# One Trainium2 core, an encoder block: Down's seven-product units spread over two column groups, features loaded in order of use, keys' transpositions kept in place

## The chip, the cores and the metric

The kernel runs on one core of a Trainium2 chip. The core has a matmul engine (PE; its weight loads are listed apart as PEld), a vector engine (DVE), a scalar engine (ACT), a general engine (POOL) and a synchronising engine (SP). SP and POOL issue the DMA transfers here; each has its own queue. Each engine works off its instructions in the order in which they stand in its queue, and semaphores make one engine wait for another.

The metric is the device time of one execution in microseconds (us). One execution was also profiled; the start times below are counted from the start of its span.

## The reference, cut to what matters

One encoder block on 256 positions of width 2048, with a memory of 256 positions. All of it is float32.

```python
mem_n = rms_norm(mem, mem_norm_g)
h = rms_norm(x, norm_g[l, 0])
...
x = x + mix @ w_out[l]
x = x + cross_attention(rms_norm(x, norm_g[l, 1]), mem_n, w_xq[l], w_xkv[l], w_xo[l])
x = x + swiglu(rms_norm(x, norm_g[l, 2]), w_gate_up[l], w_down[l])
return rms_norm(x, final_norm_g)

def swiglu(h, w_gate_up, w_down):
    gate, up = jnp.split(h @ w_gate_up, 2, axis=-1)
    return (jax.nn.silu(gate) * up) @ w_down
```

Two places of it matter below: the keys, `mem_n @ w_xkv[:, :2048]`, and Down, the product `(silu(gate) * up) @ w_down` of 256 x 5632 features with 5632 x 2048 weights. The 5632 features are 44 blocks of 128, called k = 0 to 43.

## The kernel before

**Weights.** All weights lie in device memory as one stream of slabs in the order in which they are used, 128 x 2048 float32 (1 MB) each. SP loads a slab (`raw`, line 128) into one of a few buffers. Every half of it, 128 x 1024, is then split: ACT copies it to a rounded part `wh` (line 148), and DVE subtracts that from the original, which gives the correction `wl` (line 149). A product of features and weights is three matmuls: high by high, high by low, low by high (lines 484, 485 and 486, in `part`). Features and the normed input are split in the same manner.

**Background work.** Work that isn't matmul is written as generators. `Background` (line 236) polls them after the products; a generator's `yield n` asks for n us of pause by a planner's count, and `SOON` is 0.01. So the source decides in which place of the instruction stream a step is written. The instructions of each engine are then ordered by a scheduler that goes by its own estimates; an instruction that was marked with `keep_place` (line 337) stays behind the one that was written before it on its engine. The splits of weights and of plain features in Down are kept in this manner.

**Keys** (lines 654 to 661). The first stage multiplies the normed memory by the key weights in three passes over the columns: the first has columns 0 to 1023 and fills four PSUM banks (`pg`), the second and the third have 512 columns and two banks each. There are four such banks in all. After a pass, `store_turned` (line 509) transposes each bank on DVE (line 513) into a buffer and issues four DMAs on POOL's queue that store it. The next pass takes the bank once its transposition has read it. Beside the passes, a generator computes the scale of the memory's norm: squares on ACT (line 603), their sum on DVE (line 607), and twelve small DVE operations on a 128 x 2 tile (`krc`, in `rstd_cols`, line 369). Background work of other mixers loads tables on SP's queue (lines 1373 to 1379).

**Down** (class at line 1078). The result's columns are four groups of 512. They are worked off in two plans, each for two groups. A plan is a list of slabs, two kinds of them:

- a *plain* slab holds four feature blocks k by one column group: 4 x 2 products (two row halves), 24 matmuls. Plain slabs cover k = 0 to 31, so there are eight for each column group.
- a *unit* holds two blocks k, k + 1 by both column groups, in a form with seven products in place of eight, 21 matmuls. The six units cover k = 32 to 43. A unit needs weights that are sums of blocks (DVE, line 181: one instruction of 1024 columns and two of 512) and a *form* of its two feature blocks (line 1083: four small DVE sums, the splits of both blocks, a split of the 384 summed columns). A unit reads its weights in four pieces, of 512, 1024, 1024 and 1024 columns.

Before, plan one is: the eight plain slabs of group 0, then the first unit, the first plain slab of group 1, the second unit, the second plain slab and so on to the sixth unit, and three plain slabs of group 1. After the last unit, `combine` (line 1137) adds the unit's four own banks into the result on DVE, beside the next plain slab; then `settle` (line 1162) adds the plain banks, beside the rest.

**Features.** Gate-and-up (line 941) stores its transposed output, the features, in device memory in blocks. `fetch` (line 918) brings them back: a DMA on POOL's queue into one of eleven buffers `tmp` (line 926), then a split into a slot (ACT copy at line 319, DVE subtraction at line 311), or for k = 32 and up the form. It keeps some loads ahead of the splits: `ahead` is 3 for the first sixteen features, which are fetched within gate-and-up (line 1022, started with its second group), and 6 for the rest (line 1202). Between two steps it pauses. `ready(k)` (line 1103) runs the fetch forward until `have`, the number of features done, has reached its argument; a plain slab and a unit ask for four features more than the one at hand. The first two slabs of plan one run in `start` (line 1189), while the last background work of gate-and-up ends; the rest in `begin` (line 1198).

Of the kernel before, what the change touches and what calls it, by code (L numbers as in the profile page):

```python
# [22 lines left out]
P = 128  # L23
# [4 lines left out]
FT = DFF // P  # L28
# [26 lines left out]

FORMED = 6

PLAIN = FT - 2 * FORMED


def down_plan():

    units = [("unit", PLAIN + 2 * i) for i in range(FORMED)]
    first, second = ([("plain", c, k) for k in range(0, PLAIN, 4)] for c in range(2))
    mix = lambda a, b: [x for pair in zip(a, b) for x in pair] + a[len(b):]
    one = first + [x for pair in zip(units, second) for x in pair] + second[FORMED:]
    two = first[:1] + mix(first[1:], units) + second
    return one, two

# [1 line left out]
PLANS = down_plan()  # L71

DOWN = GU // 16 + 16 * DFF // 1024

UNITS = {DOWN + i for i, x in enumerate(PLANS[0] + PLANS[1]) if x[0] == "unit"}

# [205 lines left out]
class Block:  # L282
# [223 lines left out]
                    self.bg.poll()  # L506
        return ps

    def store_turned(self, to, u, src):

        nc = self.nc
        self.bg.dve(src.shape[1])
        nc.vector.transpose(u, src)  # L513
        to = to.rearrange("(b f) t -> f b t", f=32)
        for a in range(4):
            nc.gpsimd.dma_start(to[:, :, 32 * a:32 * a + 32],  # L516
                                u[32 * a:32 * a + 32, :].rearrange("f (b t) -> f b t", t=32))
# [48 lines left out]
    def mixers(self):  # L566
# [77 lines left out]
        with tc.tile_pool(name="mid", bufs=1) as mid:  # L644
            self.dgp = mid
            gl = Gla(self, mid)
            with tc.tile_pool(name="hyp", bufs=1) as hyp, tc.tile_pool(name="k2", bufs=8) as k2:
                hy = Hyena(self, hyp, k2)

                mem0 = hy.piece()[:, 0:R + 16]  # L650
                nc.sync.dma_start(mem0, self.t["mem0"])
                self.bg.add(prepare(mid))

                for cols in ([0, 512], [1024], [1536]):
                    first = dict(parts=[[k] for k in range(KT)], before=start_m) if len(cols) > 1 else {}
                    for c, ps in zip(cols, self.gemm_rows("w_xkv", cols, h, **first)):
                        for r in range(2):
                            self.store_turned(self.kd[c:c + 512, r * P:(r + 1) * P], hy.piece(), ps[r][:, :])
                    if first:
                        for k in range(0, KT, 4):  # L660
                            self.load_x(k, 4)
                for hd in range(4):
                    for r, p in enumerate(self.gemm_rows("w_xkv", [D + hd * 512], h, start_x if hd == 3 else rows.append)[0]):
                        for c in range(2):
                            v, o = self.tmp(), (2 * hd + r) * 512 + c * R
                            nc.scalar.activation(v, p[:, c * R:(c + 1) * R], AF.Copy, scale=self.rcm[:, r:r + 1])
                            nc.gpsimd.dma_start(self.vd[:, o:o + R], v)
                self.bg.drain()

                def ev_u(i, p):  # L670
                    hy.feed(i, self.merge(p))
                    if i == 4:
                        self.bg.add(hy.convs())

                self.gemm("w_in", [UH + i * P for i in range(12)], h, ev_u)
                for r, p in enumerate(self.gemm_rows("w_in", [512], h, lambda k: k or low_rank())[0]):
                    nc.scalar.copy(gl.v[r], p)
                self.gemm("w_in", [256, 384, 0, 128], h, lambda i, p: gl.feed(i, self.merge(p)))
                self.gemm("w_in", scols[0:NSC], h, ev_s, narrow=True)
                self.bg.drain()  # L680

            with tc.tile_pool(name="glp", bufs=1) as glp:
                gl.open(glp)
                fn = Fnet(self, glp, act[20:24])
                g_gla = self.bg.add(gl.mix(act[4:8]))
                fn.feed(self.gemm_rows("w_in", [UF], h)[0])
                g_fn = self.bg.add(fn.mix(act[0:4], gl))
                self.gemm("w_in", scols[NSC:], h, lambda i, p: ev_s(i + NSC, p))
                g_sc = self.bg.add(self.group_norm(self.res[1], 2, act[20:24]))

                def ev_gate(i, p):
                    nc.scalar.activation(gl.gate[i], p[:, 0:R], AF.Silu)

                self.gemm("w_in", [1024 + i * P for i in range(4)], h, ev_gate, narrow=True)
                gl.done = True
                self.out_proj(lambda n: [self.bg.drain(g) for g in ((g_gla,), (g_fn, g_sc), ())[n]])
# [218 lines left out]
                    st.places = list(zip(held[0::2], held[1::2]))  # L915
                    d.end()

    def fetch(self, f, k0, k1, ahead, pause, form=None):

        m = {}  # L920
        for k in range(k0, k1 + ahead):
            if k < k1:
                while len(self.stored) <= k // 4:
                    yield
                m[k] = self.tmp()
                self.nc.gpsimd.dma_start(m[k], self.ff[k * P:(k + 1) * P, :])  # L926
            if k >= k0 + ahead:
                i = k - ahead
                if i >= PLAIN:
                    if i % 2:  # L930
                        form(i - 1, m.pop(i - 1), m.pop(i))
                        self.have = i + 1
                        yield pause
                    continue
                mark = self.mark()
                self.split(f[i], m.pop(i))
                self.keep_place(mark)
                self.have = i + 1
                yield pause

    def gate_up(self, sw, gp, f):

        nc, st = self.nc, self.st
        box, self.stored = {}, []
        sums = {}

        def norm():
# [69 lines left out]
        for j in range(DFF // 512):  # L1017
# [1 line left out]
            banks = [self.gbank, self.bank]  # L1019
            cs = [[banks[j % 2]() for _ in cols] for _ in range(2)]  # L1020
            if j == 1:
                early = self.bg.add(self.fetch(f, 0, EARLY, 3, 2.0))
            for i in range(8):
                if j >= NUDGE and i in (2, 4, 7):
                    self.bg.nudge(turned if i == 2 else early)
# [48 lines left out]
class Down:  # L1074
# [27 lines left out]

    def ready(self, k):
        b = self.b
        while b.have < k:
            b.bg.step(next(e for e in b.bg.q if e[0] is self.fetching))

    def part(self, key, *a):
# [5 lines left out]

    def plain(self, c, i, k0):
        for k in range(k0, k0 + 4):
            self.ready(min(len(self.f), k + 4))
            w = self.st.take("w_down", k, (c + i) * 512, 4)
            if c + i == 3 and k >= PLAIN - LATE:
                self.held.append((k, w))  # L1120
                continue
            for r in range(2):
                self.part((i, r), *self.whole(k, r), *w)
# [3 lines left out]

    def unit(self, c, k):

        self.ready(min(FT, k + 4))  # L1130
        formed = lambda n: [self.forms[k][:, a + n * P:a + (n + 1) * P] for a in (0, 384)]
        for (key, a), w in zip((("p1", self.whole(k, 0)), ((1, 0), formed(2)), ((0, 0), self.whole(k + 1, 0)),
                                ("p5", self.whole(k, 1)), ("p7", formed(1)), ("p6", formed(0)), ((0, 1), self.whole(k + 1, 1))),
# [64 lines left out]
    def begin(self, sd):  # L1198

        b = self.b  # L1200
        self.sd = sd
        self.fetching = b.bg.add(b.fetch(self.f, EARLY, FT, 6, SOON, self.form))
        one, two = PLANS
        n, self.rest = (1 + max(i for i, x in enumerate(plan) if x[0] == "unit") for plan in PLANS)
        self.run(0, one[AHEAD:n], b.gbank)
# [643 lines left out]
```

## Time and profile before

| | |
|---|---|
| runs (us) | 1461.06, 1459.96, 1461.03 |
| median (us) | 1461.03 |
| the profiled execution (us) | 1459.79 |
| its span, first to last instruction (us) | 1458.0 |
| mean granted clock of PE | 0.997 |
| weight splits on ACT, line 148 | 589 instructions, 1013 ns mean |
| weight corrections on DVE, line 149 | 589 instructions, 1175 ns mean |
| slab loads on SP | 246 of 1 MB |
| feature loads on POOL, line 926 | 44 of 128 KB |

Rows of a timeline read: start in us, duration in us, engine, line, operation, output<-input, shape; "x3" at the end joins three instructions in a row; a bracket gives the idle time of the engine before it and what ended it. Rows of windows read: window, its length, then busy us (and instructions) of PE, PEld, DVE, ACT and POOL, the granted clock of PE (1.00 is full), the busy share of the DMA engines, and GB/s. In the rows of DMA issues the last number is the median time from issue to landing. PE's neighbouring matmuls overlap in these records, and their ends are modelled.

### The profile page before, as it was taken

To read this page: it belongs to the slowest core of one execution; us is meant where nothing else is said; L and a number is where in the kernel's file an instruction comes from. 1 tells how busy PE (TensorE), PEld (TensorE's weight loads), DVE (VectorE), ACT (ScalarE), POOL (GpSimd) and SP (SyncE) were. 2 spreads that over 40 slices of the span, in tenths; PEclk is the share of its full clock that TensorE was granted. 3 is DMA by queue.
4 is the path that set the end of the run, shared out by engine and by line. 5 is a ranking of instruction groups with operands and counts; after the bars stand their busy time and mean duration, and the time that the engine had idled before them with its cause. 6 is when DMAs were issued, how large, how long until landed. Compare 5 with 4: busy or idle time off the path is not lost.

```text
span 1458.0 us, 19733 instructions
## 1 busy us (share of the span) xinstructions
PE 1441.3 (99%) x7219; PEld 1218.0 (84%) x7219; DVE 1191.4 (82%) x1748; ACT 843.7 (58%) x1252; POOL 172.3 (12%) x294
## 2 busy tenths in 40 slices
PE   9999999999999999999999999999999999899997
PEld 7878888898899888888888888888888888688886
DVE  6587768778868767877778999999999996898875
ACT  6555755466656646765565555555555564555554
POOL 0220100000000001100003344112201113100000
PEclk9999999999999999999999999999999999999999
DMA  9975654454535656545556767666666656465554
GB/s 349 346 263 196 220 210 154 165 180 161 191 130 206 214 178 224 173 171 191 183 203 202 279 240 246 207 219 221 243 218 243 238 204 223 155 229 179 226 203 144
DMA packets 57393, 307.16 MB, mean 211 GB/s; under 512 B 9773, under 2 KB 11470, under 8 KB 25680
## 3 DMA queue, kind: packets, MB, share of 16 engines
q1 hardware_dynamic: 45920, 281.11, 54.3%
q0 software_dynamic: 10944, 24.14, 5.4%
q8 instruction: 56, 0.92, 0.3%
q10 hardware_dynamic: 432, 0.66, 0.1%
q14 instruction: 41, 0.34, 0.1%
HBM read 291.71 MB, written 14.16 MB: 210 GB/s over the span
## 4 chain that ended last, share of the span: by engine, by line
PE 94%; issue 2%; DVE 1%; DMA 1%; POOL 1%; ACT 1%; SPq 0%; DVEq 0%; POOLq 0%; ACTq 0%
PE pg L433 18%; PE pg L485 13%; PE pg L486 13%; PE pg L484 13%; PE pg L434 10%; PE pm L485 6%; PE pm L484 6%; PE pm L486 6%; PE pm L1350 1%; DMA tmp<-hidden 1%; DVE wl L149 1%; PE pg L430 1%; PE pg L431 1%; PE pm L881 1%; PE pm L854 1%
## 5 line engine op out<-in xcount | busy, mean ns | idle before, releaser
L148 ACT CAST wh<-raw 128x1024 fp32r<-128x1024 f32 (+1 forms) x589 | 589.3, 1013 | 475.8 <-PE pg L486 147.8
L149 DVE TENSOR_TENSOR wl<-raw,wh 128x1024 fp32r<-128x1024 f32 (+1 forms) x589 | 681.4, 1175 | 179.4 <-ACT wh L148 173.7
L433 PE MATMUL pg<-act,wh 128*128 128x512 f32 x1104 | 387.6, 393 | 0.0
L434 PE MATMUL pg<-act,wl 128*128 128x256 f32 x1216 | 340.7, 280 | 0.0
L485 PE MATMUL pg<-wl,act 128*128 128x512 f32 (+1 forms) x689 | 268.3, 389 | 3.0 <-DVE wl L149 3.0
L484 PE MATMUL pg<-wh,act 128*128 128x512 f32 (+1 forms) x689 | 268.8, 391 | 0.5 <-ACT wh L148 0.5
L486 PE MATMUL pg<-wh,act 128*128 128x512 f32 (+1 forms) x689 | 268.2, 389 | 0.0
L433 PEld LDWEIGHTS pg<-act,wh 128*128 128x128 f32 x1104 | 207.4, 188 | 44.9
L434 PEld LDWEIGHTS pg<-act,wl 128*128 128x128 f32 x1216 | 228.6, 188 | 0.8 <-DVE wl L149 0.5
L485 PEld LDWEIGHTS pg<-wl,act 128*128 128x128 f32 x689 | 129.5, 188 | 31.3 <-DVE wl L149 4.8
L484 PEld LDWEIGHTS pg<-wh,act 128*128 128x128 f32 x689 | 129.5, 188 | 28.2 <-issue 0.8
L486 PEld LDWEIGHTS pg<-wh,act 128*128 128x128 f32 x689 | 129.4, 188 | 27.3 <-issue 0.4
L484 PE MATMUL pm<-wh,act 128*128 128x512 f32 x318 | 124.5, 391 | 1.2 <-ACT act L319 1.2
L486 PE MATMUL pm<-wh,act 128*128 128x512 f32 x318 | 124.4, 391 | 0.6 <-DVE act L311 0.6
L485 PE MATMUL pm<-wl,act 128*128 128x512 f32 x318 | 124.5, 391 | 0.0
L181 DVE TENSOR_TENSOR raw<-raw 128x1024 f32<-128x1024 f32 x129 | 111.6, 865 | 2.9
L516 POOL DMA_DIRECT2D hidden<-u x88 | 56.8, 653 | 152.5 <-DVE u L513 130.4
L484 PEld LDWEIGHTS pm<-wh,act 128*128 128x128 f32 x318 | 60.1, 189 | 14.2 <-ACT act L319 1.6
L486 PEld LDWEIGHTS pm<-wh,act 128*128 128x128 f32 x318 | 60.1, 189 | 13.5 <-DVE act L311 1.0
L485 PEld LDWEIGHTS pm<-wl,act 128*128 128x128 f32 x318 | 60.0, 189 | 12.5
L1062 POOL DMA_DIRECT2D xrows<-tmp x64 | 37.0, 585 | 184.2 <-DVE rc L315 126.6
L926 POOL DMA_DIRECT2D tmp<-hidden x44 | 24.5, 561 | 151.4 <-DVE f L311 87.4
(353 smaller groups left out, 1773.0 us busy)
## 6 DMA issues: line engine op xcount, KB each, us to landing
raw<-in_W SPq DMA_DIRECT2D x246, 1024.0 KB, 5.0
raw<-in_W SPq DMA_DIRECT2D x11, 512.0 KB, 7.2
hidden<-u POOLq DMA_DIRECT2D x88, 64.0 KB, 4.6
tmp<-hidden POOLq DMA_DIRECT2D x44, 128.0 KB, 4.7
res<-in_xT SPq DMA_DIRECT2D x8, 512.0 KB, 8.3
k<-in_mem SPq DMA_DIRECT2D x8, 256.0 KB, 6.6
k<-in_x SPq DMA_DIRECT2D x8, 256.0 KB, 8.9
keys<-k POOLq DMA_DIRECT2D x32, 64.0 KB, 5.7
```

Of the source, the lines that this page charges most:

```text
L148: nc.scalar.copy(wh[:, a:b], r[:, a:b])
L149: nc.vector.tensor_tensor(out=wl[:, a:b], in0=r[:, a:b], in1=wh[:, a:b].bitcast(F32), op=ALU.subtract)
L181: op = lambda out, a, b, what=ALU.subtract: nc.vector.tensor_tensor(out=out, in0=a, in1=b, op=what)
L430: self.nc.tensor.matmul(p[:, 0:R], wh, slot[:, 0:R], start=start, stop=False)
L433: self.nc.tensor.matmul(p[:, :], wh, slot[:, :], start=start, stop=False)
L434: self.nc.tensor.matmul(p[:, 0:R], wl, slot[:, 0:R], start=False, stop=stop)
L484: self.nc.tensor.matmul(p, hi, wh, start=start, stop=False)
L485: self.nc.tensor.matmul(p, hi, wl, start=False, stop=False)
L486: self.nc.tensor.matmul(p, lo, wh, start=False, stop=stop)
L516: nc.gpsimd.dma_start(to[:, :, 32 * a:32 * a + 32], u[32 * a:32 * a + 32, :].rearrange("f (b t) -> f b t", t=32))
L926: self.nc.gpsimd.dma_start(m[k], self.ff[k * P:(k + 1) * P, :])
L1062: nc.gpsimd.dma_start(to[:, :, c:c + 32], u[32 * a:32 * a + 32, :].rearrange("t (b f) -> t b f", f=32))
```

## The change

Three things change.

1. Plan one's order. Group 0's eight plain slabs and group 1's eight stand in a row, and the units are put in after the fifth, seventh, ninth, eleventh, thirteenth and fourteenth of them (`AFTER`, counted from 0). Plan two, the number of slabs and their contents stay; so does the layout of each slab, while the stream's order follows the plan.
2. `INNER` lists the features in the order in which plan one first uses them: 0 to 19, 32, 33, 20 to 27, 34, 35, 28 to 31, 36 and so on. `fetch` goes by such a list, keeps eight loads ahead instead of six, pauses 0.8 instead of 0.01 after a plain feature and 3.0 after a form; `have` counts features in that order, and `ready(k)` runs the fetch until four more than k's place are done. The sixteen features fetched early are the same. Since the last unit now stands before two plain slabs only, `combine` runs beside the first and `settle` beside the second.
3. The transpositions of the keys are kept at their written place on DVE. In the built program, DVE's queue at the end of the first pass then reads: a weight correction, the sum of line 607, the twelve operations on `krc`, a weight correction, the four transpositions, a weight correction. Before, the first transposition stood after the second of the twelve operations, the other three after the third, and both weight corrections and the other nine operations behind them. At the end of the second pass two weight corrections stood behind the two transpositions; now they stand ahead of them.

```diff
@@ -55,6 +55,8 @@
 
 FORMED = 6
 
+AFTER = (4, 6, 8, 10, 12, 13)
+
 PLAIN = FT - 2 * FORMED
 
 
@@ -63,7 +65,9 @@
     units = [("unit", PLAIN + 2 * i) for i in range(FORMED)]
     first, second = ([("plain", c, k) for k in range(0, PLAIN, 4)] for c in range(2))
     mix = lambda a, b: [x for pair in zip(a, b) for x in pair] + a[len(b):]
-    one = first + [x for pair in zip(units, second) for x in pair] + second[FORMED:]
+    one = []
+    for n, x in enumerate(first + second):
+        one += [x] + [units[i] for i, a in enumerate(AFTER) if a == n]
     two = first[:1] + mix(first[1:], units) + second
     return one, two
 
@@ -71,6 +75,8 @@
 PLANS = down_plan()
 
 DOWN = GU // 16 + 16 * DFF // 1024
+
+INNER = list(dict.fromkeys(k for x in PLANS[0] for k in (range(x[2], x[2] + 4) if x[0] == "plain" else range(x[1], x[1] + 2))))
 
 UNITS = {DOWN + i for i, x in enumerate(PLANS[0] + PLANS[1]) if x[0] == "unit"}
 
@@ -506,11 +512,14 @@
                     self.bg.poll()
         return ps
 
-    def store_turned(self, to, u, src):
+    def store_turned(self, to, u, src, keep=False):
 
         nc = self.nc
         self.bg.dve(src.shape[1])
+        mark = self.mark()
         nc.vector.transpose(u, src)
+        if keep:
+            self.keep_place(mark)
         to = to.rearrange("(b f) t -> f b t", f=32)
         for a in range(4):
             nc.gpsimd.dma_start(to[:, :, 32 * a:32 * a + 32],
@@ -655,7 +664,7 @@
                     first = dict(parts=[[k] for k in range(KT)], before=start_m) if len(cols) > 1 else {}
                     for c, ps in zip(cols, self.gemm_rows("w_xkv", cols, h, **first)):
                         for r in range(2):
-                            self.store_turned(self.kd[c:c + 512, r * P:(r + 1) * P], hy.piece(), ps[r][:, :])
+                            self.store_turned(self.kd[c:c + 512, r * P:(r + 1) * P], hy.piece(), ps[r][:, :], True)
                     if first:
                         for k in range(0, KT, 4):
                             self.load_x(k, 4)
@@ -915,33 +924,34 @@
                     st.places = list(zip(held[0::2], held[1::2]))
                     d.end()
 
-    def fetch(self, f, k0, k1, ahead, pause, form=None):
+    def fetch(self, f, ks, ahead, pause, form=None):
 
         m = {}
-        for k in range(k0, k1 + ahead):
-            if k < k1:
+        for n in range(len(ks) + ahead):
+            if n < len(ks):
+                k = ks[n]
                 while len(self.stored) <= k // 4:
                     yield
                 m[k] = self.tmp()
                 self.nc.gpsimd.dma_start(m[k], self.ff[k * P:(k + 1) * P, :])
-            if k >= k0 + ahead:
-                i = k - ahead
+            if n >= ahead:
+                i = ks[n - ahead]
                 if i >= PLAIN:
                     if i % 2:
                         form(i - 1, m.pop(i - 1), m.pop(i))
-                        self.have = i + 1
-                        yield pause
+                        self.have += 2
+                        yield 3.0
                     continue
                 mark = self.mark()
                 self.split(f[i], m.pop(i))
                 self.keep_place(mark)
-                self.have = i + 1
+                self.have += 1
                 yield pause
 
     def gate_up(self, sw, gp, f):
 
         nc, st = self.nc, self.st
-        box, self.stored = {}, []
+        box, self.stored, self.have = {}, [], 0
         sums = {}
 
         def norm():
@@ -1019,7 +1029,7 @@
             banks = [self.gbank, self.bank]
             cs = [[banks[j % 2]() for _ in cols] for _ in range(2)]
             if j == 1:
-                early = self.bg.add(self.fetch(f, 0, EARLY, 3, 2.0))
+                early = self.bg.add(self.fetch(f, INNER[:EARLY], 3, 2.0))
             for i in range(8):
                 if j >= NUDGE and i in (2, 4, 7):
                     self.bg.nudge(turned if i == 2 else early)
@@ -1102,7 +1112,7 @@
 
     def ready(self, k):
         b = self.b
-        while b.have < k:
+        while b.have < min(INNER.index(k) + 5, len(INNER)):
             b.bg.step(next(e for e in b.bg.q if e[0] is self.fetching))
 
     def part(self, key, *a):
@@ -1114,7 +1124,7 @@
 
     def plain(self, c, i, k0):
         for k in range(k0, k0 + 4):
-            self.ready(min(len(self.f), k + 4))
+            self.ready(k)
             w = self.st.take("w_down", k, (c + i) * 512, 4)
             if c + i == 3 and k >= PLAIN - LATE:
                 self.held.append((k, w))
@@ -1127,7 +1137,7 @@
 
     def unit(self, c, k):
 
-        self.ready(min(FT, k + 4))
+        self.ready(k + 1)
         formed = lambda n: [self.forms[k][:, a + n * P:a + (n + 1) * P] for a in (0, 384)]
         for (key, a), w in zip((("p1", self.whole(k, 0)), ((1, 0), formed(2)), ((0, 0), self.whole(k + 1, 0)),
                                 ("p5", self.whole(k, 1)), ("p7", formed(1)), ("p6", formed(0)), ((0, 1), self.whole(k + 1, 1))),
@@ -1199,7 +1209,7 @@
 
         b = self.b
         self.sd = sd
-        self.fetching = b.bg.add(b.fetch(self.f, EARLY, FT, 6, SOON, self.form))
+        self.fetching = b.bg.add(b.fetch(self.f, INNER[EARLY:], 8, 0.8, self.form))
         one, two = PLANS
         n, self.rest = (1 + max(i for i, x in enumerate(plan) if x[0] == "unit") for plan in PLANS)
         self.run(0, one[AHEAD:n], b.gbank)
```

## The prediction

> **What bounds the kernel now.** I read the page first, then the span cut into windows, then the stretches in which PE is not full.
>
> ```profile
> span 1458.0 us, 19733 instructions
> PE 1441.3 (99%) x7219; PEld 1218.0 (84%) x7219; DVE 1191.4 (82%) x1748; ACT 843.7 (58%) x1252; POOL 172.3 (12%) x294
> PE 94%; issue 2%; DVE 1%; DMA 1%; POOL 1%; ACT 1%; SPq 0%; DVEq 0%; POOLq 0%; ACTq 0%
> ...
> 1250.00:1300.00 50.00, 47.27 (x196) 37.34 (x197) 47.54 (x75) 29.80 (x43) 1.63 (x3) 0.97 0.50 181
> 1300.00:1350.00 50.00, 50.00 (x223) 41.40 (x222) 43.34 (x52) 28.40 (x36) 0.00 (x0) 1.00 0.55 200
> ```
>
> PE is busy for 1441.3 of 1458.0 us and is 94% of the chain that ended last. So the kernel is bound by matmuls, and no edit that keeps them can win more than PE's gaps. The windows (columns: length, busy time and instructions of PE, PEld, DVE, ACT and POOL, granted clock, DMA share, GB/s) place a gap at 1250 to 1300, where Down's seven-product units start; at 1300 to 1350, still in Down, PE is full. The other place is the keys, at 73 to 76 us.
>
> **Down: what the old order loses.** These are PE's matmuls around the switch from group 0's plain slabs to the units, three ACT copies, and windows.
>
> ```profile
> 1210.09 0.39 PE L484 MATMUL pm<-wh,act 128*128 128x512 f32 x1
> 1226.41 0.39 PE L484 MATMUL pm<-wh,f 128*128 128x512 f32 x1
> ...
> 1248.22 0.39 PE L486 MATMUL pm<-wh,f 128*128 128x512 f32 x1
> 1249.83 0.50 PE L484 MATMUL pm<-wh,act 128*128 128x512 f32 x1 [1.22 <-ACT act L319]
> 1251.12 0.51 PE L486 MATMUL pm<-wh,act 128*128 128x512 f32 x1 [0.56 <-DVE act L311]
> 1261.84 0.50 PE L485 MATMUL pg<-wl,act 128*128 128x512 f32 x1 [1.35 <-DVE wl L149]
> 1264.32 0.49 PE L485 MATMUL pg<-wl,s 128*128 128x512 f32 x1 [0.82 <-DVE wl L149]
> 1264.88 0.40 PE L484 MATMUL pm<-wh,act 128*128 128x512 f32 x1
> ...
> 1248.12 0.41 ACT L319 CAST act<-tmp 128x256 fp32r<-128x256 f32 x1 [3.05 <-DMA tmp<-hidden]
> 1256.16 0.41 ACT L319 CAST act<-tmp 128x256 fp32r<-128x256 f32 x1 [3.81 <-DMA tmp<-hidden]
> ...
> 1248.45:1264.89 16.44, 12.49 (x44) 8.82 (x44) 12.92 (x26) 10.94 (x22) 1.63 (x3) 0.90 0.30 105
> 1248.17:1251.58 3.41, 1.63 (x6) 0.72 (x6) 2.07 (x5) 3.36 (x8) 0.22 (x1) 1.00 0.32 103
> 1251.58:1254.99 3.41, 3.41 (x10) 2.63 (x9) 3.41 (x9) 0.71 (x2) 1.34 (x3) 0.50 0.90 322
> 1258.41:1261.82 3.41, 2.08 (x9) 1.11 (x7) 3.41 (x7) 1.84 (x4) 0.00 (x0) 1.00 0.00 0
> ```
>
> 1210.09 and 1226.41 begin the first and the fourth slab, so a plain slab of 24 matmuls takes 16.32 / 3 = 5.44 us, 0.2267 us each. From 1248.22 to 1264.88 there are 44 matmuls (the window's x44 counts both ends), 43 steps: 43 x 0.2267 = 9.75 us of the 16.66 us that pass. So 6.9 us are lost. The four bracketed waits are 3.95 of it; the clock at 0.50 for 3.41 us, after a window in which PE was busy for 1.63 us, costs half of that, 1.7; restarts and small gaps are the rest. Some 0.3 us on either side of the stretch makes **7.5 us** in all. Cause: ACT stands still for 3.05 and 3.81 us behind features that have not landed, since forms and plain features are fetched in numerical order, and the copies and sums of the first units queue behind them. I find no gap of PE from 1264.88 to 1300.
>
> **Down: what the new order costs.** The matmuls are the same in number and kind, only in other places, so PE's work costs nothing more. The same holds for DVE's and ACT's. What moves is when the forms and weight sums fall due. These rows price them.
>
> ```profile
> 1241.28 0.29 DVE L311 TENSOR_TENSOR e<-tmp 128x128 f32<-128x128 f32 x1 [3.54 <-DMA tmp<-hidden]
> 1236.99 0.76 DVE L311 TENSOR_TENSOR f<-tmp,f 128x256 fp32r<-128x256 f32 x2
> 1270.14 0.68 DVE L181 TENSOR_TENSOR raw<-raw 128x512 f32<-128x512 f32 x1
> 1270.74 0.28 DVE L315 SCALAR_TENSOR_TENSOR e<-tmp 128x128 f32<-128x128 f32 x1
> 1232.26 1.08 POOL L926 DMA_DIRECT2D tmp<-hidden  x2 [1.64 <-DVE f L311]
> ...
> tmp<-hidden POOLq DMA_DIRECT2D x2, 128.0 KB, 2.9
> ...
> raw<-in_W SPq DMA_DIRECT2D x246, 1024.0 KB, 5.0
> tmp<-hidden POOLq DMA_DIRECT2D x44, 128.0 KB, 4.7
> ...
> 1235.52 5.74 DMA tmp<-hidden
> ```
>
> One instruction of DVE starts some 0.08 us before the last one ends (1270.14 + 0.68 against 1270.74), so in a row of them a 512 sum counts 0.6, a small sum 0.2, a split of 256 columns 0.34. The row with 2.9 us is the median landing of the loads issued between 1232 and 1233.5; the last row is the longest one in the chain of waits.
>
> Unit 0 now stands after five plain slabs: 1210.09 + 5 x 5.44 = 1237.29. Its 21 matmuls read four pieces of weights; the correction of the fourth piece is first read by the 17th matmul, at 1237.29 + 16 x 0.2267 = 1240.92. On DVE's new queue the first sum of forms 34/35 stands ahead of that piece and waits for a load. From it on DVE needs 2 x 0.2 (that sum and another), 2 x 0.6 (two 512 sums of weights), 4 x 0.34 (splits of plain features) and 2 x 1.16 (corrections of the third and fourth pieces; 2.32 for two in a row of the keys below) = 5.3 us. The load now issues at about 1232.4. Landing in 2.9 us as then and there (1235.3), DVE is held by its own queue till about 1235.8 and the piece is 0.1 late; landing in the usual 4.7 (1237.1) it is 1.5 late. I take 0.2, since the 2.9 row is from the same time and queue.
>
> Unit 1 follows two plain slabs later, at about 1253. Its slab's load is issued once DVE has left unit 0's fourth piece, about 1241.1, and lands at 1246.1 by the 5.0 row. The load of feature 37, issued about 1244.8 and behind it, lands about 1249.5, and its ACT copy stands ahead of unit 1's second piece. From there: that copy 0.4, the weight copy 1.0 (2.00 for two, in the keys' rows), its correction 1.16, two sums 1.2, the form of 36/37 some 2 (four sums, two splits, one split of 384 columns at perhaps 0.5), third and fourth pieces 2.3 = 8.1, so 1257.6 where 1253 + 3.63 = 1256.6 is wanted: 1.0 late. Unit 2 I put at 0.6, an estimate: it comes after as many slabs, and unit 1's wait has given its loads a microsecond. The sum is 1.8, with 0.2 for each of three restarts **2.4 us**. Ends: 1.0 (unit 0 and unit 1 on time but for half a microsecond each) and 5.5 (each load 1 us later). Then Down gains 7.5 - 2.4 = 5.1; I take 4.7, because the slabs loaded after the units come in the same window as the features. Ends: 6.5 and 2. Nothing in the new tail loses PE time: combining group 0 now runs beside one plain slab and settling beside another, the cover that the row 1300 to 1350 shows full with 43 of 50 us on DVE; without it, two 512 adds at 0.7 would be bare. A copy of feature 33 now waits in gate_up for PE, ahead of a weight copy that is held by DVE anyway; nothing.
>
> **Keys.** Here the change takes a wait away and makes another.
>
> ```profile
> 48.89 0.17 DVE L378 TENSOR_SCALAR krc<-krc 128x2 uint32<-128x2 uint32 x1
> 48.97 0.71 DVE L513 STREAM_TRANSPOSE k<-pg 128x512 f32<-128x512 f32 x1
> 49.64 2.08 DVE L513 STREAM_TRANSPOSE k<-pg 128x512 f32<-128x512 f32 x3
> 50.80 0.39 PE L484 MATMUL pg<-wh,act 128*128 128x512 f32 x1
> 51.64 2.32 DVE L149 TENSOR_TENSOR wl<-raw,wh 128x1024 fp32r<-128x1024 f32 x2
> 53.88 0.15 DVE L315 SCALAR_TENSOR_TENSOR krc<-krc 128x2 f32<-128x2 f32 x1
> 55.44 0.16 DVE L315 SCALAR_TENSOR_TENSOR krc<-krc 128x2 f32<-128x2 f32 x1
> ...
> 61.23 3.37 SPq L128 DMA_DIRECT2D raw<-in_W  x3
> 68.94 2.00 ACT L148 CAST wh<-raw 128x1024 fp32r<-128x1024 f32 x2 [1.03 <-DMA raw<-in_W]
> 73.19 1.40 DVE L513 STREAM_TRANSPOSE k<-pg 128x512 f32<-128x512 f32 x2 [2.02 <-PE pg L486]
> 75.75 0.50 PE L485 MATMUL pg<-wl,act 128*128 128x512 f32 x1 [1.47 <-DVE wl L149]
> ```
>
> Before, the first transposition ran at 48.97, in the middle of the small krc operations, and its PSUM bank was free before pass 2's first matmul at 50.80. Kept at its written place, it stands behind all of krc and one weight correction: 48.89 + 0.2 to the next, 0.2 more, then the nine operations that took 53.88 to 55.60, 1.72: 51.0; + 1.16 = 52.15; + 0.71 = 52.85. Pass 2 starts at about 52.95: 2.15 us of idle PE, 2.26 with the restart. The other three transpositions, 0.69 apart, keep pace with a bank per three matmuls (0.68).
>
> At the end of pass 2 the order turns in favour: two corrections now stand ahead of the transpositions which waited 2.02 us for PE. The 1.47 of idle PE at 75.75 goes, 1.7 with its restart. But ACT's chain is 2.2 us later, and behind one of its squares SP's queue holds a table, and then pass 3's first slab: issued at about 66.9, not 61.23. With the old 7.6 us to landing it is there at 74.5, + 1.0 + 1.16 = 76.7 against about 76 wanted (74.1, where the old stall began, and the shift): 0.7 late; with the 5.0 row it is in time. I take 0.35. Keys: 2.26 - 1.73 + 0.35 = **+0.9**, ends +0.5 and +1.3, if the clock stays at 1.00.
>
> The clock may not: a window with 1.63 us of PE went to half speed, one with 2.08 did not (rows above). A stall of 2.15 leaves 1.26 busy in a window of 3.41 us that holds it whole, 1.3 to 2.3 in one that cuts it. The Trainium skill, "TensorE: Matmul & The Clock Gate", section "🔬 Part 1: The HAM clock gate (the "warmup" mystery)", gives the cold state "after ≥1 idle window (~3.4µs)"; by that no stall of 2 us would cost a clock, and the sum would stand. The trace disagrees: 0.50 followed a window with 1.63 us of busy PE.
>
> **Sum.** Against the profiled execution, 1459.79 us (span 1458.0 and 1.8 around it): -4.7 + 0.9 = -3.8, so 1456.0. The median of the runs, 1461.03, lies 1.24 above that execution; 1457.2.
>
> **Rivals.**
> (a) Pass 2's stall drops the clock: 3.41 us at half speed, +1.7: 1458.9. For it the 1.63 row, against it the 2.08 row.
> (b) Slower: the form loads come late. From 5.7 us between issue and landing (the 5.74 row) on, DVE's queue stands behind the load at unit 0: 1232.4 + 5.74 + 5.3 = 1243.4 against 1240.92, 2.5 late. Unit 1, waited for by ACT behind slab and load each about a microsecond later, is 2.4 late, unit 2 about 2. With restarts 0.7 and a half-speed window 1.7 that is 9.3 against the 7.5 lost before; with keys +0.9 and their own half-speed window +1.7 it is 4.4 more: 1465.4. For it: the loads are issued closer together now, eight ahead; against: 2.9 and 4.7.
> (c) The stalls of units 0 to 2 hide entirely: -7.5 + 0.9: 1454.4. Against it: DVE's 5.3 us queue.
> (d) Spreading only moves the gap: the first units stall as before, keys +0.9: 1461.9. For it: the first unit still comes with fetches not done.
>
> **How the numbers follow.** Forecast 0.45, (a) 0.2, (b) 0.15, (c) 0.1, (d) 0.1. A measurement here tells about 0.2% or 2.9 us: faster is below 1458.1, slower above 1464.0. Two thirds of the forecast with (c) and a third of (a) are faster: about 0.52; (b) with a little of (d) 0.17 is slower; the rest 0.31. The range, 1454.6 to 1462.2, reaches from (c) past (d) and leaves (b) out.
>
> **What would show it.** Right: PE idle about 2.1 us at 51 to 53 with DVE's transposition as its releaser, no wait at the end of keys' pass 2 or one under a microsecond, Down's 1237 to 1275 with waits summing to 1 to 3 us and the clock at 1.00. Wrong: waits of ACT or DVE for loaded features over 3 us there, a clock of 0.50 after 53, or a gap at the end of group 1, where combining meets one slab alone.

## The result and the profile after

| | before | after |
|---|---|---|
| median of nine runs each (us) | 1460.0 | 1456.9 |
| lowest and highest | 1459.38 to 1461.09 | 1455.38 to 1460.82 |
| the profiled execution | 1459.79 | 1457.18 |
| its span | 1458.0 | 1455.3 |

The ratio of after to before is 0.9979, 95% interval 0.9969 to 0.9989. That is 3.1 us faster. The median of before had stood at 1461.03 with the three runs that were known first; with six more it is 1460.0.

The page of after, its span, busy times and the shares of the chain that ended last:

```profile
span 1455.3 us, 19732 instructions
PE 1440.2 (99%) x7219; PEld 1217.8 (84%) x7219; DVE 1192.2 (82%) x1748; ACT 844.1 (58%) x1252; POOL 172.2 (12%) x294
...
PE 96%; DVE 2%; ACT 1%; issue 0%; DMA 0%; SPq 0%; ACTq 0%; DVEq 0%
```

The work of each engine is what it was (DVE 1192.2 against 1191.4). What changed is who PE waits for: DMA and "issue", 3% of the chain before, have left it. Line numbers have moved: the weight splits are now lines 154 and 155, the product 490 to 492, the transposition 520, the copy and split of features 325 and 317.

PE's waits in the timeline of after, at the keys and in Down:

```profile
52.78 0.54 PE L490 MATMUL pg<-wh,act 128*128 128x512 f32 x1 [1.99 <-DVE k L520]
53.11 0.63 PE L491 MATMUL pg<-wl,act 128*128 128x512 f32 x1
...
1258.40 0.50 PE L491 MATMUL pg<-wl,act 128*128 128x512 f32 x1 [0.87 <-DVE wl L155]
1260.57 0.50 PE L491 MATMUL pg<-wl,s 128*128 128x512 f32 x1 [0.51 <-DVE wl L155]
...
1275.79 0.50 PE L490 MATMUL pg<-wh,s 128*128 128x512 f32 x1 [0.38 <-ACT wh L154]
```

Before had one wait at the keys (75.75) and four in Down from 1249 to 1265, 3.95 us. Now there are one at the keys, elsewhere, and three in Down, 1.76 us. The one at 52.78 is new, and the matmul behind it takes 0.63 us instead of 0.39: the clock fell. Windows of after:

```profile
49.62:53.04 3.42, 1.43 (x7) 0.92 (x6) 3.21 (x10) 1.64 (x3) 0.10 (x1) 1.00 0.96 348
53.04:56.45 3.41, 3.41 (x9) 2.64 (x9) 3.02 (x6) 0.00 (x0) 3.41 (x6) 0.50 0.94 276
1200.00:1250.00 50.00, 49.96 (x221) 41.05 (x220) 40.90 (x62) 27.13 (x41) 13.91 (x24) 1.00 0.67 229
1250.00:1300.00 50.00, 48.24 (x211) 38.92 (x210) 45.30 (x71) 29.58 (x42) 2.17 (x4) 1.00 0.59 221
```

PE was busy for 1.43 of the 3.42 us up to 53.04, and the next 3.41 us ran at a granted clock of 0.50. In Down the clock stayed at 1.00 and the number of matmuls from 1250 to 1300 rose from 196 to 211.

To see where the difference arises, I matched the starts of the matmuls in the two traces by their number and subtracted. The lag of after is -0.18 us at the 200th matmul (46 us), +1.89 at the 400th, +1.85 at the 6200th (1212 us) and -2.65 at the 6600th; it stays there to the end. So the keys cost **2.07 us**, Down's first plan gained **4.50**, and the rest of the span did nothing. The same two differences (200th to 400th, "keys"; 6200th to 6800th, "Down") are given for each experiment below. The first 24 us vary by up to 1.8 us between these traces, so they are left out of both.

### The profile page after: what moved, and what is told of

It reads as the page before. It is cut to its first block, busy times and chain, and to the rows that moved or that the text cites. A ratio compares the mean times of both kernels' runs of the same rounds, so it can differ in the third digit from the quotient of the medians.

```text
span 1455.3 us, 19732 instructions
## 1 busy us (share of the span) xinstructions
PE 1440.2 (99%) x7219; PEld 1217.8 (84%) x7219; DVE 1192.2 (82%) x1748; ACT 844.1 (58%) x1252; POOL 172.2 (12%) x294
## 4 chain that ended last, share of the span: by engine, by line
PE 96%; DVE 2%; ACT 1%; issue 0%; DMA 0%; SPq 0%; ACTq 0%; DVEq 0%
PE pg L439 19%; PE pg L490 13%; PE pg L491 13%; PE pg L492 13%; PE pg L440 10%; PE pm L490 7%; PE pm L492 7%; PE pm L491 7%; PE pm L1360 1%; DVE wl L155 1%; PE pg L436 1%; PE pg L437 1%; PE pm L890 1%; PE pm L863 1%; ACT wh L154 0%
```

## Experiments

Times are medians; each ratio is to runs of the kernel before on the same chip (median 1460.37 for the first four, 1459.65 and 1459.66 for the others). "Under before" and "over before" are meant against these. Behind the last two columns stands one trace of each kernel. Seven kernels, the change and six of the runs below, have the same plan and the same order of features; their Down still differs by up to 1.6 us, for a reason worked out further below (when one load landed), so smaller differences in that column are not taken for effects.

| run | median (us) | ratio, 95% interval | keys | Down |
|---|---|---|---|---|
| Down alone | 1455.97 | 0.9970, 0.9958 to 0.9981 | -0.03 | -5.15 |
| keys alone | 1461.51 | 1.0008, 0.9999 to 1.0017 | +2.03 | +0.45 |
| first pass free, later passes kept | 1453.84 | 0.9958, 0.9945 to 0.9970 | -1.80 | -4.23 |
| features in numerical order | 1464.26 | 1.0024, 1.0014 to 1.0034 | -0.03 | +3.84 |
| six ahead, no pauses | 1455.03 | 0.9968, 0.9955 to 0.9980 | -0.01 | -5.06 |
| old plan, new fetch | 1458.31 | 0.9989, 0.9980 to 0.9998 | -0.03 | -1.75 |
| second to fourth unit one slab later | 1455.30 | 0.9969, 0.9957 to 0.9980 | -1.81 | -1.27 |
| eight ahead, short pauses | 1454.43 | 0.9960, 0.9947 to 0.9974 | -1.81 | -3.56 |
| later passes kept, six ahead, no pauses | 1453.85 | 0.9961, 0.9948 to 0.9973 | -1.80 | -4.80 |
| first four units one slab later | 1457.97 | 0.9990, 0.9981 to 0.9999 | -1.81 | -1.20 |
| three ahead | 1456.12 | 0.9976, 0.9967 to 0.9984 | -0.03 | -4.38 |

### Down alone and keys alone

Down alone takes the flag away that keeps the keys' transpositions:

```diff
-self.store_turned(self.kd[c:c + 512, r * P:(r + 1) * P], hy.piece(), ps[r][:, :], True)
+self.store_turned(self.kd[c:c + 512, r * P:(r + 1) * P], hy.piece(), ps[r][:, :])
```

> The change to Down and its features alone; the keys' transpositions are free again. By the working of the prediction Down is worth about 4.5 us (the lag of PE's matmuls against before went from +1.85 to -2.65 across Down's first plan), so 4.5 under the kernel before, and all runs close together since no stall at pass 2 is left to touch the clock. Rival: the keys' edit carries part of the gain, then this is less than 3.1 under, the gain of the whole change.

4.4 us under before. The keys' stage is before's again, to 0.03 us. The gain is Down's, and by the traces the whole change gains less than this part of it; the intervals of the two ratios overlap. My second half held less well: the runs spread over 3.3 us, from 1454.14 to 1457.41, all with a recorded mean clock of 0.998 or 0.999, so the touched clock is not the only thing that spreads them.

Keys alone is the kernel before with `store_turned`'s new argument and nothing else:

```diff
+        mark = self.mark()
         nc.vector.transpose(u, src)
+        if keep:
+            self.keep_place(mark)
```

> The keys' edit alone on the kernel before. Theory: a stall of 2.27 us at pass 2's start, minus 1.7 at pass 3's, so 0.4 to 0.6 us over before where the clock stays, and 1.4 more, about 2.1 over, in the runs where the stall drops it; runs spread over some 2 us. Rival: the edit gains, as the wait of 1.47 us at 75.75 goes: 1.5 under.

1.1 us over before by the medians, between the two cases of the theory; the interval touches no change. In its trace the keys cost 2.03 us. PE in the timeline of keys alone:

```profile
53.60 0.48 PE L484 MATMUL pg<-wh,act 128*128 128x512 f32 x1 [1.98 <-DVE k L514]
53.91 0.60 PE L485 MATMUL pg<-wl,act 128*128 128x512 f32 x1
54.30 0.63 PE L486 MATMUL pg<-wh,act 128*128 128x512 f32 x1
```

The same stall and the same half clock behind it as in the kernel with the whole change: two profiled executions of two kernels with this stall, and in both the clock dropped. The rival, that this edit gains, falls.

### Only the later passes kept

```diff
-..., hy.piece(), ps[r][:, :], True)
+..., hy.piece(), ps[r][:, :], not first)
```

> The whole change, but the transpositions of the first pass are free, those of the second and third are kept. Theory: no stall at 52, and no wait of 1.47 us at the end of pass 2: 1.7 under Down alone, so 6.2 under the kernel before. Rival: without the two microseconds of shift the second pass's end meets a slab that has not landed, and the wait stays in another form: the same as Down alone.

6.5 us under before, 2.1 under Down alone (the two intervals overlap, but the traces separate the stages), and the keys' part is -1.80. DVE in its timeline, and the window over the keys:

```profile
48.29 0.17 DVE L384 TENSOR_SCALAR krc<-krc 128x2 uint32<-128x2 uint32 x1
48.37 0.71 DVE L520 STREAM_TRANSPOSE k<-pg 128x512 f32<-128x512 f32 x1
49.01 0.12 DVE L385 TENSOR_SCALAR krc<-krc 128x2 int32<-128x2 int32 x1
49.05 2.08 DVE L520 STREAM_TRANSPOSE k<-pg 128x512 f32<-128x512 f32 x3
...
50.00:100.00 50.00, 50.00 (x220) 40.28 (x219) 35.60 (x72) 27.60 (x43) 17.74 (x29) 1.00 0.84 290
```

The transpositions of the first pass again run ahead of the small operations, and PE is full from 50 to 100 us, where before had 48.53 of 50. So the keys' edit is two edits: at the later passes it takes a stall away, worth 1.8, and at the first it makes one.

### What in Down carries the gain

Numerical order, with the new plan and free keys:

```diff
-INNER = list(dict.fromkeys(k for x in PLANS[0] for k in ...))
+INNER = list(range(FT))
```

> Down's new plan with the features fetched in numerical order (keys free). Theory: the order of use is what makes the early units possible; unit 0 at 1237 then stands behind twelve more plain features and their loads, a stall of 4 to 8 us that takes the 4.5 away: 0 to 4 over before. Rival: spreading the units is what gains, the order of the loads is not: 3 to 4.5 under before.

Slower than before by 3.9 us; Down costs 3.84 in the trace. PE in its timeline:

```profile
1240.77 0.50 PE L490 MATMUL pm<-wh,act 128*128 128x512 f32 x1 [2.29 <-ACT act L325]
1242.25 0.80 PE L492 MATMUL pm<-wh,act 128*128 128x512 f32 x1 [0.57 <-DVE act L317]
1251.25 0.68 PE L490 MATMUL pg<-wh,s 128*128 128x512 f32 x1 [2.98 <-ACT wh L154]
```

Unit 0 now stands where its features are not ready: its first matmul waits for the ACT copy of feature 32. An early unit without early features loses 9 us against one that has them (3.84 against -5.15). Part of it may be the clock: it was at 0.50 from 1241.17 to 1247.99 and from 1251.41 to 1254.82, each time after a wait of PE; how much these 10.2 us cost beside the waits is not shown.

The old plan with the new depth and pauses:

```diff
-for n, x in enumerate(first + second):
-    one += [x] + [units[i] for i, a in enumerate(AFTER) if a == n]
+one = first + [x for pair in zip(units, second) for x in pair] + second[FORMED:]
```

> The old plan (group 0's slabs, then units and slabs in turn) with the new fetch: eight ahead, pauses 0.8 and 3.0, keys free; the order of use is then the numerical one. Theory: the old loss at the switch, 7 us, comes from units that start one slab apart with their forms all at once; two loads more ahead shorten the wait for the first form by some 2 us: 0 to 2.5 under before. Rival: depth and pauses are the cure, not the plan: 4 or more under before.

1.3 us under before, Down -1.75. Depth and pauses alone are not the cure. The old place of the waits remains: they sum to 3.95 us as before, with 1.35 us for the split of a feature at 1253.77 the longest of them. The clock stayed at 1.00.

The new plan with the old depth and pauses:

```diff
-b.fetch(self.f, INNER[EARLY:], 8, 0.8, self.form)
+b.fetch(self.f, INNER[EARLY:], 6, SOON, self.form)
...
-yield 3.0
+yield pause
```

> Down alone (keys free), features in order of use, but fetched as before: six loads ahead, pauses of 0.01. Theory: the order carries the gain, depth and pauses only place the copies and forms between the weights; within 1.5 us of Down alone, so 3 to 5.5 under before. Rival: eight ahead and the pauses are needed, since the early forms' loads come too late with six (the wait for loaded features, 3.9 us in all in the changed kernel, grows): less than 2 under before.

Down is -5.06 against -5.15 of Down alone: once order and plan are there, this depth and these pauses do nothing that can be told. Fewer loads ahead still:

```diff
-b.fetch(self.f, INNER[EARLY:], 8, 0.8, self.form)
+b.fetch(self.f, INNER[EARLY:], 3, 0.8, self.form)
```

> Down alone (keys free) with three feature loads ahead instead of eight, pauses as changed: the loads of the forms come late, the prediction's slower rival made on purpose. If loads that are late by 1 us or more stall units 0 to 2 as I worked out, each unit pays 1.5 to 2.5 us and the clock may drop: 0 to 4 over before, 5 to 8 over Down alone. Rival: forms have slack of a few us, and it costs under 2 against Down alone.

The rival expectation held: Down -4.38, 0.8 less than with eight ahead. ACT's waits for loaded features from 1190 to 1320, in the list of waits of this kernel and of Down alone:

```profile
ACT act L325 <- DMA tmp<-hidden: 4.6, 2, 3.2
```

```profile
ACT act L325 <- DMA tmp<-hidden: 3.8, 2, 2.5
```

The longest wait grew by only 0.7 us, and that is not the setting's doing: the edit did not make the loads late. Less each trace's own lag, the loads of features 20 to 39 go out at the same times with three, six and eight ahead, with and without pauses, to 0.03 us in all seven kernels of this plan and order. POOL's queue waits there for DVE's splits, which free the buffers (the row at 1246.94 further below). So no setting of depth or pauses that was tried moved these loads, and the price of loads late by a whole microsecond at each unit was not measured.

### Attempts at the waits that are left

All four keep the later passes only. Units after the 5th, 8th, 10th, 12th, 13th and 14th slab:

```diff
-AFTER = (4, 6, 8, 10, 12, 13)
+AFTER = (4, 7, 9, 11, 12, 13)
```

> As with the late passes kept and the first free, with units after the 5th, 8th, 10th, 12th, 13th and 14th slab: all plain features come before the second unit. Theory: the waits at units 1 and 2 (1.7 and 0.5 us lost in the changed kernel) come from features that the plain slab between needs as well; with three slabs between units 0 and 1 they shrink below 0.7 in all, 1 to 2 under the same kernel with the change's places. Rival: the last three units one slab apart bring DVE's queue to its limit, as the old plan did, and the loss moves there: 0 or worse.

4.4 us under before where the change's places had 6.5, with overlapping intervals; Down falls to -1.27, outside the 1.6 us of the seven kernels. Not the last units pay, as the rival had it, but unit 1. ACT and PE in its timeline:

```profile
1258.77 0.51 ACT L333 CAST s<-e 128x384 fp32r<-128x384 f32 x1 [1.20 <-DVE e L317]
1259.19 1.04 ACT L154 CAST wh<-raw 128x1024 fp32r<-128x1024 f32 x1
...
1260.28 0.56 PE L490 MATMUL pg<-wh,act 128*128 128x512 f32 x1 [1.88 <-ACT wh L154]
1261.67 0.80 PE L491 MATMUL pg<-wl,act 128*128 128x512 f32 x1 [0.82 <-DVE wl L155]
```

No plain feature is left to fetch between these units, so the forms of the next ones move up, and ACT's copy of one stands ahead of unit 1's weights and waits for DVE. The clock was at 0.50 for 6.83 us from 1260.57 on as well, so part of what is lost there may be its own. The first four units one slab later:

```diff
-AFTER = (4, 6, 8, 10, 12, 13)
+AFTER = (5, 7, 9, 11, 12, 13)
```

> Units after the 6th, 8th, 10th, 12th, 13th and 14th slab (later passes kept, first free, eight ahead). Theory: loads of 36 and 37 are then due one slab later as well, but so are they issued, since DVE's splits free their buffers; the wait at unit 1 stays at 1 to 2 us, within 1 of the run with the change's places. Rival: a slab more before the first unit is 5.4 us of cover, and the waits go: 1.5 to 2.5 under it.

Worse than both expectations: 1.7 us under before, Down -1.20, with waits at units 0 and 1, 4.5 us in all. DVE at its unit 0:

```profile
1239.88 0.29 DVE L317 TENSOR_TENSOR e<-tmp 128x128 f32<-128x128 f32 x1 [3.25 <-DMA tmp<-hidden]
```

DVE's queue stands for 3.25 us behind a form's feature, as it did for 3.54 in the kernel before. Later units do not make earlier features: here the load of feature 34 went out 2.5 us later than in the seven kernels (less the lag), and took 5.93 us to land instead of 2.4 to 2.7. Short pauses with eight ahead:

```diff
-b.fetch(self.f, INNER[EARLY:], 8, 0.8, self.form)
+b.fetch(self.f, INNER[EARLY:], 8, SOON, self.form)
```

> As with the late passes kept and the first free, pauses for plain features 0.01 instead of 0.8, eight ahead. Theory: the load of the second unit's features, issued 3.6 us later than I had estimated, moves forward with the copies; the 1.7 us at unit 1 shrinks: 0.5 to 1.5 under the same kernel with pauses. Rival: copies and splits crowd the weights of gate-and-up's end and unit 0: 0 to 2 over it.

5.2 us under before where the run with pauses had 6.5, with overlapping intervals; Down -3.56 in the trace. The theory's gain is not there, and its premise was wrong: the load issued 3.6 us later than I had estimated (1248.41 against 1244.8) is that of feature 38. The one I had estimated, of feature 37, had gone out at 1246.94, and shorter pauses did not move it. Last, the two best parts together (first pass free, six ahead, no pauses):

> The parts that did best together: first pass's transpositions free, later ones kept, new plan, order of use, six loads ahead without pauses. Theory: the keys' 1.7 us and Down's 4.6 us are in different stages and add up: 6.3 or more under before, equal to or up to 0.5 under the run with eight loads and pauses. Rival: the depth matters only in the noise: the two within 0.3.

5.8 us under before: the stages add up (-1.80 and -4.80), but this is not told apart from the kernel with eight ahead, 1453.84. Both lie below the change itself (ratios 0.9958 and 0.9961 against 0.9979), with intervals that just meet its own, 0.9969 to 0.9989.

## Why the prediction was right, and where not

**What bounds.** PE's gaps were the whole prize. The keys and Down's first plan hold all of the difference; 1000 us of matmuls between them moved by 0.04.

**Down's gain.** Predicted 4.7, measured 4.50 (5.15 in Down alone, 3.56 to 5.06 in the five other kernels with this plan and order). Of the waits worked out in advance:

- Unit 0, predicted 0.2 late with DVE held by its own queue: DVE reached form 34's first sum at 1237.61 without waiting for a load, where I had 1235.8 and the lag of 1.85 comes on top. The unit's 17th matmul started 0.42 us after the one before instead of 0.23, and with the slower next one the unit lost 0.33 (lag 1.85 at the 6330th matmul, 2.18 at the 6340th).

```profile
1237.61 0.28 DVE L317 TENSOR_TENSOR e<-tmp 128x128 f32<-128x128 f32 x1
...
1240.68 1.09 DVE L317 TENSOR_TENSOR f<-tmp,f 128x256 fp32r<-128x256 f32 x3
```

- Unit 1, predicted 1.0 and 0.2 for the restart. Measured: 0.87 + 0.51 of waits, 1.9 by the distances between the matmuls' starts (1.25 and 0.34, 0.90 and 0.34 instead of 0.23). This is the mis-sized term of Down's sum. The path is the one named: ACT's copy of feature 37 stands ahead of the second piece and starts as its load lands.

```profile
1246.94 0.55 POOL L936 DMA_DIRECT2D tmp<-hidden  x1 [3.93 <-DVE f L317]
1248.41 1.08 POOL L936 DMA_DIRECT2D tmp<-hidden  x2 [0.93 <-DVE f L317]
...
1252.24 0.41 ACT L325 CAST act<-tmp 128x256 fp32r<-128x256 f32 x1 [2.85 <-DMA tmp<-hidden]
```

  Counted in the order of use, the load of feature 37 is the one at 1246.94. Less the lag of 1.85 that is 1245.1, where I had about 1244.8; it landed 5.28 us later, where I had 4.7. So ACT's copy comes 0.9 later than worked out, and the unit loses 0.7 more. The working behind it holds: 8.1 us after the copy's start is 1260.3, and the unit's 17th matmul starts at 1260.57.
- Unit 2, put at 0.6 and a restart by an estimate: the wait at 1275.79, 0.64 by the distances.
- The tail, costed at nothing: the lag is -2.65 at the 6600th matmul and at the 7200th. Combining beside one slab costs PE nothing.

The three units lose 2.9 us where 2.4 were put down, out of 7.5 in before; 4.6 is left, and the lag says 4.50. That 4.7 comes so near is partly luck: it holds 0.4 taken off for the slabs loaded after the units, and no loss shows there (the lag is -2.64 at the 6478th matmul and -2.65 at the 6600th), while unit 1 cost 0.7 more than worked out.

The landing of that one load sets what Down gains. In the seven kernels it goes out at the same place, to 0.01 us, units 0 and 2 lose the same to 0.1 us, and unit 1 follows the landing (its loss is taken from the starts of the matmuls 6389 to 6412):

| kernel | load of feature 37, issue to landing (us) | lost at unit 1 (us) | Down |
|---|---|---|---|
| six ahead, no pauses | 4.45 | 1.4 | -5.06 |
| Down alone | 4.49 | 1.3 | -5.15 |
| later passes kept, six ahead, no pauses | 4.84 | 1.7 | -4.80 |
| three ahead | 5.09 | 2.1 | -4.38 |
| the change | 5.28 | 2.0 | -4.50 |
| first pass free, later passes kept | 5.59 | 2.2 | -4.23 |
| eight ahead, short pauses | 6.21 | 2.9 | -3.56 |

Why it lands sooner or later, these runs do not show.

The 7.5 us that before loses are not a sum of waits and a separate price of the clock, as the prediction's first working has it. In keys alone, whose Down is before's, the clock stayed at 1.00 there; PE's waits were 5.01 us instead of 3.95, and Down lost no less, 0.45 us more:

```profile
1250.00:1270.00 20.00, 15.09 (x59) 10.26 (x59) 15.10 (x29) 12.68 (x23) 2.51 (x5) 1.00 0.39 133
```

**Keys.** The stall at pass 2 was worked out as 2.15 us with a first matmul at 52.95; it came at 52.78, and the lag jumped by 2.15 in that step (-0.18 at the last matmul of pass 1, 1.97 at the next). DVE's queue reads as described, with the correction and then all four transpositions behind the small operations:

```profile
50.70 0.16 DVE L321 SCALAR_TENSOR_TENSOR krc<-krc 128x2 f32<-128x2 f32 x1
50.78 1.23 DVE L155 TENSOR_TENSOR wl<-raw,wh 128x1024 fp32r<-128x1024 f32 x1
51.92 2.50 DVE L520 STREAM_TRANSPOSE k<-pg 128x512 f32<-128x512 f32 x4
```

The end of pass 2 gave 1.77 back (3.70 to 1.93) where I had 1.73. Pass 3's first slab was to be 0.35 late: 0. SP's queue behaved as described: the slab's load went out at 68.35, 1.45 after the 66.9 that I had. PE was 1.4 us later by then than my stall alone made it (lag 3.70 against 2.26), by the half clock; that this delayed the load too is likely and not shown. It landed in the 5.0 us of the better of my two cases, since ACT's copy starts 5.04 later:

```profile
68.35 12.41 SPq L134 DMA_DIRECT2D raw<-in_W  x5
73.39 2.00 ACT L154 CAST wh<-raw 128x1024 fp32r<-128x1024 f32 x2 [3.13 <-DMA raw<-in_W]
```

The step that failed is a chance, not a price: I gave the drop of the clock 0.2 as rival (a), and both traces of kernels with the stall show it, at 1.7 us with the restart (lag 1.97 to 3.68) against 1.7 and 0.1. So the profiled execution is the rival's: Down nearly as forecast and keys at +2.07, 2.6 us under before's own profiled execution (1457.18 to 1459.79) where the forecast had 3.8 and rival (a) 2.1.

The runs that were not profiled have a recorded mean clock, and a half-clock stretch of 3.41 us takes 0.0012 off it (1.7 of 1455 us). In the sixty runs of the eight kernels whose traces show no such stretch at the keys or in Down, it is 0.998 or 0.999. In after, four of nine runs have 0.995 to 0.997, with a median of 1457.98 us, and five have 0.998 or 0.999, with 1456.32. In keys alone seven of eleven have 0.996 or 0.997 (1461.88) and four more than that (1460.63); a stretch in Down would look the same there. A single run is not settled by its rounded mean, but the clock seems to drop in about half of the runs, not in a fifth and not in all.

So the five runs of after are 3.7 us under before's 1460.0, where the forecast had 3.8, and the four 2.0 under, where rival (a) had 2.1. The median of all nine came out within 0.3 us of the predicted one by luck: three runs of before had put its median a microsecond too high, and the runs that dropped the clock went the other way. The prediction's own rows could have told that 0.2 was too little: if a window of 3.41 us falls anywhere with equal chance against a stall of 2.15, PE is busy for less than 1.63 us of it in 0.6 of the places. This is an estimate, from the row with 1.63 and the prediction's own window.

**The clock.** The Trainium skill, "TensorE: Matmul & The Clock Gate", section "🔬 Part 1: The HAM clock gate (the "warmup" mystery)", asks for a whole idle window of about 3.4 us before the cold state. Here waits of 1.99 and 1.98 us were enough in the two traces, with PE busy for 1.43 of 3.42 us in the changed kernel; the measurement decides.

**The rivals.** (b), the slower one, rested on DVE's queue standing behind late loads. The mechanism exists: with numerical order, and with the first four units one slab later, it took 9 and 3 us from Down (3.84 against -5.15, the half clock in it; -1.20 against -4.23). In the changed kernel the loads of unit 0's forms were in time, and the price I gave it for three units was not met by any run with this plan and order. (c), nothing lost at the units, is refuted by 1258.40 to 1275.79, (d) by the lag. One sum of the chances was wrong: two thirds of 0.45, 0.1 and a third of 0.2 make 0.47, not 0.52.

## What to carry to other kernels

Order loads by the first use of what they bring, and move the work that needs them together with the order: the new places with the old order of loads lost 3.8 us, deeper loading with pauses at the old places gained 1.8, and the new places with the new order 3.6 to 5.2, whatever the depth. Check in the trace that a setting moved what it was meant to move: three loads ahead and eight gave the same issue times. When an instruction is pinned in its queue, look at what then stands ahead of it at each of its places; the same flag was worth 1.8 us at one pass and cost 2.15 us, and in both traces a drop of the clock, at another. A margin between two medians of three runs can be off by a microsecond; matching matmuls between two traces tells where the time of these two executions differs far more closely than the total does, but one stage of one kernel can itself differ by a microsecond and more from execution to execution.

## What was not expected of the hardware

A gap of 2 us in PE's work cost 3.85 us in all (lag -0.18 to 3.68): 2.15 in the gap, and 1.7 in eight matmuls that started 0.43 us apart instead of 0.23, in two traces of two, and by the recorded clocks in about half of the runs. In before, a window with 1.63 us of busy PE had led to the same and one with 2.08 not; now one with 1.43 has.

One 128 KB load, issued at the same place of the program to 0.01 us, landed after 4.45 to 6.21 us in seven executions, and a gain of 3.56 to 5.15 us followed it.
